# Two value products in one visit of the array, one copy for both, and other queues at the two passages of a hybrid attention layer

## The chip, the cores and the metric

The kernel runs on one core of a Trainium2 chip. The core has five engines with queues of their own: TensorE (PE), VectorE (DVE), ScalarE (ACT), GpSimd (POOL) and SyncE (SP). Each works through its queue in order; they meet through semaphores. SP here issues DMAs only; ACT and GpSimd issue some too. The metric is the device time of one execution in microseconds, and the median of several runs is compared.

## The reference

One layer of a decoder on 4096 tokens of width 1024, all in float32:

```python
h = rms_norm(x, norm_gain)                       # (4096, 1024)
qa, ka, va, ga, qr, kr, vr, gr = split(h @ w_in) # 4 x 512, 2 x 256, 2 x 512 columns
# 8 heads of 64: causal sliding window attention, three branches
for window, dilation in ((128, 1), (512, 4), (2048, 16)):
    s = q . k * 64**-0.5       # a query sees the 128 steps before it, at that dilation
    m, p = max(s), exp(s - max(s)); den = sum(p)
    o, lse = (p . v) / den, m + log(den)
attn = sum over branches of softmax(lse) * o
# 4 heads, key 64, value 128: retention in chunks of 128 with decay, then a norm per head
ret = group_norm(retention(qr, kr, vr)) * ret_gain
mixed = concat(silu(ga) * attn, silu(gr) * ret)
out = rms_norm(x + mixed @ w_out, final_gain)
```

Its products have a float32 result; the kernel splits operands of the large ones into a high part (hi) and a rest (lo) and adds three products (`mm3`, lines 46 to 50: hi·hi, hi·lo, lo·hi).

## The kernel before

It has three phases. **Phase 1** projects the tokens in 8 blocks of 512 to q, k, r (the q and k of retention) and the values, rotates q, k and r, and stores them to DRAM (`dr_q`, `dr_k`, `dr_r`, `dr_v`). **Phase 2** is the attention of 8 heads, with retention in 32 chunks as filler between. **Phase 3** computes the gates `g`, the mixed values `m`, the output projection `po` and the last norm.

In phases 1 and 2 the order of every engine is the order in which the program is written (`manual_schedule`). In phase 2 `attention()` is a generator that yields once per slot, and it returns the slot's planned cost in ns; `filler()` yields pieces of retention and of its values' projection with their costs; between two slots the planner takes pieces from the filler as long as the sum of costs lies below an even share per slot (`slot`). Phase 3's order is set by the framework.

A head has 24 groups (48 half-groups, one per slot; 384 slots in all): a group is four blocks of 128 queries, each against up to 256 keys, for one branch. In slot t the program writes, in this order: the scores of half-group t (`qk_bank`, tile S, L667), the transposes of the exponentials of half-group t−2 (`t_bank`, tile T, L704), in every second slot the product with the values of the group that ended two slots before (`pv_group`, tile O, L737), in the slots between the copy of O out of PSUM by ACT (`o_copy`: os for branches 0 and 1, L752; ob with a stride for branch 2, L759), the exponentials of half-group t−1 (`exp_row`, tile P, ACT, L695), a copy of T to SBUF (pt; ACT L714 for the second bank, DVE L716 for the first), and the row maxima of half-group t (`row_max`, DVE, L688). S has two PSUM buffers, T two, O one. The product uses the two halves of 64 columns of PE's array for the two banks.

At the passage from phase 1 to phase 2, SP's queue holds the first three and a half thousand columns of k for head 0 (`load_k`, L445, tile kk), the last stores of k, and the next chunk of x (hr, L423) for retention's values. The values' chunk (vch, L1037) is made from hr through hc.

At the passage from phase 2 to phase 3, the last head's statistics (st, L779, stored by SP to `dr_st` and loaded again to `raw`) lead to the branch weights (`dr_w`); the gates' weights wg0 and wg1 and the output weights wo are split to hi (ACT) and lo (GpSimd, or for every second wo DVE); e is the silu of a gate (ACT L1190) and m what goes into the projection.

Of the kernel before, what the change touches and what calls it, by code (L numbers as in the profile page):

```python
# [22 lines left out]
TRN = 109  # L23
# [7 lines left out]
H = 8  # L31
# [21 lines left out]
class Split:  # L53
# [22 lines left out]
    def split(self, j, lo_engine=None):  # L76
# [10 lines left out]
        self.nc.scalar.activation(hi, raw, AF.Copy)  # L87
# [27 lines left out]
def phase1(tc, io, dr, right, ahead):  # L115
# [5 lines left out]
    with ExitStack() as ctx:  # L121
# [203 lines left out]
        for b in range(NBLK):  # L325
# [40 lines left out]
            if last:  # L366
# [4 lines left out]
                kk = load_k(nc, kka, dr, 0, cols=slice(0, S - BLK))  # L371
# [172 lines left out]
def phase2(tc, io, dr, right, ahead, early3, raw, M):  # L544
# [3 lines left out]
    with ExitStack() as ctx:  # L548
# [34 lines left out]
        PT = [c2.tile([128, 8, 128], F32, name=f"pt{i}") for i in range(2)]  # L583
# [141 lines left out]
        def pv_group(it):  # L725

            h, br = it["h"], it["br"]
            o = psO.tile([128, 512], F32, tag="O", name="O2")
            ops = [pv_ops(it, bank) for bank in range(2)]
            for x in range(-max(map(len, ops)), 0):  # L730
                for bank in range(2):
                    if -x > len(ops[bank]):
                        continue
                    r, n, a, m, c0 = ops[bank][x]
                    idx = r * NB_OF[br] + n
                    need_v(h, br, idx // 8)
                    nc.tensor.matmul(  # L737
                        o[64 * bank : 64 * bank + 64, c0 : c0 + 128 * m],
                        vt[h, br, idx // 8][:, idx % 8, :],
                        it["pt"][:, a : a + m, :].rearrange("p a b -> p (a b)"),  # L740
                        start=-x == len(ops[bank]),
                        stop=x == -1,
                        skip_group_check=True,
                    )
            it["O"] = o

        def o_copy(it):
            h, br = it["h"], it["br"]
            r, n = it["blocks"][0]
            if br < 2:  # L750
                ob = osp.tile([128, 256], F32, tag="os", name="os2")
                nc.scalar.activation(ob, it["O"][:, :256], AF.Copy)  # L752
                c0 = n * 128 if br == 0 else r * 1024 + n * 128
                later(2, store_o, h, br, c0, 512, ob)
            else:
                if r % 4 == 0:
                    obuf[h] = ob16p.tile([128, 1024], F32, tag="ob16", name="ob16")

                nc.scalar.activation(  # L759
                    obuf[h].rearrange("p (m r) -> p r m", r=4)[:, r % 4, :], it["O"][:, :256], AF.Copy  # L760
                )
                if r % 4 == 3:
                    later(2, store_o, h, br, (r // 4) * 1024, 2048, obuf[h])

# [697 lines left out]
```

## Time and profile before

| what | value |
|---|---|
| median of three runs | 2415.1 us (2414.91 to 2417.89) |
| the profiled execution | 2416.7 us |
| its span | 2414.9 us |
| PE busy in the span | 2342.5 us, 97% |
| DVE, ACT, GpSimd busy | 62%, 41%, 30% |
| granted TensorE clock, mean | 0.988 |

Engine names are PE, PEld (weight loads), DVE, ACT, POOL; SPq, ACTq and POOLq are DMAs issued by that engine. A row of the timeline has the start in us from the start of the span, the duration, the engine, the line of the program, the operation, the tiles as out<-in, the shape and the number of instructions joined in it; in brackets stands the idle time of that engine before it and what ended the wait. A row of a group has the busy time in us, the mean of one in ns, and the idle time before them with its releasers. Rows of windows give a stretch and the busy time of each engine in it.

### The profile page before, as it was taken

What the parts mean: (1) busy time and instruction counts of PE and PEld (TensorE: products, weight loads), DVE (VectorE), ACT (ScalarE), POOL (GpSimd) and SP (SyncE); (2) the same over time, 40 slices, a digit from 0 to 9 for tenths busy, and PEclk for the clock granted to TensorE, in tenths of its full rate; (3) what the DMA queues carried; (4) which work ended last, traced back from release to release, by engine and by line L of the source; (5) the groups of instructions that cost most, each with busy time, mean ns of one, the idle gap of its engine ahead of it and who ended that gap; (6) DMA issues with size and microseconds to landing.
All of it is one profiled execution on the core that took longest, in us unless ns stands there. A gap on an engine that the chain in (4) does not pass through costs nothing. (4 is left out here: it accounts for less than half of the span.)

```text
span 2414.9 us, 41800 instructions
## 1 busy us (share of the span) xinstructions
PE 2342.5 (97%) x14568; PEld 1986.1 (82%) x14568; DVE 1485.8 (62%) x3923; ACT 990.0 (41%) x2865; POOL 725.0 (30%) x765
## 2 busy tenths in 40 slices
PE   7999999999997999999999999998899999999998
PEld 5778888888885888888888887877789899999997
DVE  5643543543534878787887879786665565665654
ACT  4322222222211666666666666667222222222221
POOL 5312112112112535353544535455221121121110
PEclk9999999999998999999999999999999999999999
DMA  6343343343356766758586765746575656656553
GB/s 192 130 145 107 133 144 107 133 144 111 129 147 202 165 163 139 181 131 189 131 180 148 169 156 131 176 125 196 143 182 154 145 171 152 145 168 154 142 153 92
DMA packets 404259, 362.59 MB, mean 150 GB/s; under 512 B 191848, under 2 KB 334824, under 8 KB 398928
## 3 DMA queue, kind: packets, MB, share of 16 engines
q1 hardware_dynamic: 389408, 332.91, 52.6%
q10 hardware_dynamic: 14112, 25.43, 3.4%
q8 instruction: 115, 1.88, 0.3%
q0 software_dynamic: 528, 1.58, 0.2%
q14 instruction: 96, 0.79, 0.1%
HBM read 241.18 MB, written 118.64 MB: 149 GB/s over the span
## 5 line engine op out<-in xcount | busy, mean ns | idle before, releaser
L688 DVE CUSTOM_DVE_ANT_0 S<-S,mask 128x256 f32<-128x256 f32 (+1 forms) x768 | 308.4, 402 | 156.7 <-PE S L667 123.5
L695 ACT ACTIVATE P<-S,nm 128x256 f32<-128x256 f32 (+1 forms) x768 | 337.2, 449 | 46.9 <-DVE nm L688 43.9
L50 PE MATMUL g<-h,wg 128*128 128x256 f32 x1024 | 290.6, 284 | 0.0
L704 PE MATMUL T<-ident,P 128*128 128x128 f32 x1368 | 213.3, 274 | 0.0
L49 PE MATMUL po<-wo,m 128*128 128x512 f32 x512 | 200.6, 392 | 0.0
L50 PEld LDWEIGHTS g<-h,wg 128*128 128x128 f32 x1024 | 197.1, 192 | 0.0
L737 PE MATMUL O<-pt,v 128*64 128x128 f32 (+1 forms) x1968 | 195.8, 325 | 0.0
L667 PE MATMUL S<-kk,qc 128*128 128x256 f32 x1024 | 186.9, 306 | 6.8 <-issue 2.8
L48 PE MATMUL po<-wohi,m 128*128 128x512 f32 x448 | 178.9, 399 | 6.9 <-ACT m L40 5.4
L1251 POOL TENSOR_TENSOR rs<-v,mhalf 128x1 f32<-128x1 f32 x32 | 17.5, 547 | 547.0 <-DVE v L1249 384.9
L667 PEld LDWEIGHTS S<-kk,qc 128*128 128x128 f32 x1024 | 150.0, 191 | 34.7 <-issue 17.5
L50 PE MATMUL po<-wohi,m 128*128 128x512 f32 x448 | 176.9, 396 | 0.2 <-DVE m L41 0.2
L172 POOL TENSOR_TENSOR sq<-sq,sq 128x512 f32<-128x512 f32 x56 | 76.3, 1362 | 331.4 <-ACT sq L168 331.4
L435 POOL TENSOR_TENSOR hc<-hr,hc 128x512 fp32r<-128x512 f32 x64 | 85.9, 1343 | 289.3 <-ACT hc L434 149.6
L737 PEld LDWEIGHTS O<-pt,v 128*64 128x64 f32 x1968 | 121.2, 137 | 60.3 <-issue 31.2
L704 PEld LDWEIGHTS T<-ident,P 128*128 128x128 f32 x1368 | 163.8, 141 | 0.2 <-ACT wg0hi L87 0.2
L695 ACT ACTIVATION_READ_ACCUMULATOR P<-S,nm 128x1 f32 x768 | 157.5, 205 | 0.0
L48 PE MATMUL g<-h,wg1hi 128*128 128x256 f32 x512 | 145.9, 286 | 4.6 <-ACT e L1190 4.5
L40 ACT ACTIVATE m<-e 128x256 fp32r<-128x256 f32 x128 | 53.1, 417 | 234.5 <-DVE e L1197 137.8
L49 PE MATMUL g<-h,wg1hi 128*128 128x256 f32 x512 | 146.9, 287 | 0.9 <-DVE h L483 0.7
L48 PE MATMUL g<-h,wg0hi 128*128 128x256 f32 x512 | 144.8, 283 | 1.8 <-ACT e L1190 1.8
L49 PE MATMUL g<-h,wg0hi 128*128 128x256 f32 x512 | 144.9, 283 | 0.0
(212 smaller groups left out, 6120.7 us busy)
## 6 DMA issues: line engine op xcount, KB each, us to landing
q<-dr_q SPq DMA_DIRECT2D x128, 256.0 KB
hr<-in_xT_dram SPq DMA_DIRECT2D x64, 512.0 KB
wb<-dr_w SPq DMA_DIRECT2D x128, 192.0 KB
o<-dr_o SPq DMA_DIRECT2D x192, 128.0 KB
v<-dr_v SPq DMA_DIRECT2D x94, 256.0 KB
xt<-in_xT_dram SPq DMA_DIRECT2D x64, 256.0 KB
dr_q<-hl SPq DMA_DIRECT2D x32, 512.0 KB
dr_k<-hl SPq DMA_DIRECT2D x32, 512.0 KB
```

The costliest lines, as they stand in the source:

```text
L40: nc.scalar.activation(dst[:, 0], src, AF.Copy)
L48: nc.tensor.matmul(out, wh, xh, start=first and i == 0, stop=False)
L49: nc.tensor.matmul(out, wh, xl, start=False, stop=False)
L50: nc.tensor.matmul(out, wl, xh, start=False, stop=last and i == n - 1)
L172: nc.gpsimd.tensor_tensor(sums[b], sums[b], sq, ALU.add)
L435: nc.gpsimd.tensor_tensor(hc[:, :, 1, :], src, hc[:, :, 0, :].bitcast(F32), ALU.subtract)
L667: nc.tensor.matmul(s[:, j * 256 : (j + 1) * 256], qq[h, t, half][:, off : off + 128] if br == 0 else it["q"][:, t, i, :], rhs, start=(j == ...
L688: nc.vector.tensor_tensor_reduce(sv, sv, mask[:, it["br"], c0:256], 1.0, BIG, ALU.add, ALU.min, accum_out=nm[:, col : col + 1])
L695: nc.scalar.activation(it["P", i // 2][:, i % 2, c0:256], sv, AF.Exp, bias=nm[:, col : col + 1], scale=-1.0, accum_out=den[:, col : col + 1])
L704: nc.tensor.transpose(t[:, j * 128 : (j + 1) * 128], it["P", bank][:, j // 2, j % 2 * 128 : j % 2 * 128 + 128], ident)
L737: nc.tensor.matmul(o[64 * bank : 64 * bank + 64, c0 : c0 + 128 * m], vt[h, br, idx // 8][:, idx % 8, :], it["pt"][:, a : a + m, :].rearran ...
L1251: nc.gpsimd.tensor_tensor(rs, v, mhalf, ALU.pow)
```

## The change

**The products of values.** `pv_group` becomes `pv_pair`: in every fourth slot (t % 4 == 2) the products of two groups are issued one behind the other, into one PSUM bank [128, 2, 256]. `o_copy` follows in the next slot, one ACT instruction of 512 columns for both. There are three PT tiles in place of two. The planned cost of a pair is 190 ns less than that of two groups, and an even share per slot falls accordingly.

**The passages.** The first load of k is issued by GpSimd in place of SP. The tile st is taken from the pool that also holds raw, and so are the tiles rb of phase 3. The last head's reloads of statistics are issued by ACT, from phase 3's start. Two loads of rt at the start of phase 3 are issued by GpSimd. All lo parts of wo are made by GpSimd, and the hi casts of wg0 by DVE in place of ACT.

```diff
@@ class Split @@
-    def split(self, j, lo_engine=None):
+    def split(self, j, lo_engine=None, hi_engine=None):
...
-        self.nc.scalar.activation(hi, raw, AF.Copy)
+        if hi_engine is None:
+            self.nc.scalar.activation(hi, raw, AF.Copy)
+        else:
+            hi_engine.tensor_copy(hi, raw)
         engine.tensor_tensor(self.lo[j], raw, hi.bitcast(F32), ALU.subtract)
@@ phase1 @@
-                kk = load_k(nc, kka, dr, 0, cols=slice(0, S - BLK))
+                kk = load_k(nc, kka, dr, 0, nc.gpsimd.dma_start, cols=slice(0, S - BLK))
@@ phase2 @@
-        PT = [c2.tile([128, 8, 128], F32, name=f"pt{i}") for i in range(2)]
+        PT = [c2.tile([128, 8, 128], F32, name=f"pt{i}") for i in range(3)]
...
-        def pv_group(it):
-            h, br = it["h"], it["br"]
-            o = psO.tile([128, 512], F32, tag="O", name="O2")
-            ops = [pv_ops(it, bank) for bank in range(2)]
...
-            it["O"] = o
+        def pv_pair(its):
+            o = psO.tile([128, 2, 256], F32, tag="O", name="O2")
+            for y, it in enumerate(its):
+                h, br = it["h"], it["br"]
+                ops = [pv_ops(it, bank) for bank in range(2)]
...
+                            o[64 * bank : 64 * bank + 64, y, c0 : c0 + 128 * m],
...
+            return o
-        def o_copy(it):
...
-                ob = osp.tile([128, 256], F32, tag="os", name="os2")
-                nc.scalar.activation(ob, it["O"][:, :256], AF.Copy)
-                c0 = n * 128 if br == 0 else r * 1024 + n * 128
-                later(2, store_o, h, br, c0, 512, ob)
+        def o_copy(its, o):
...
+                ob = osp.tile([128, 2, 256], F32, tag="os", name="os2")
+                nc.scalar.activation(ob, o, AF.Copy)
+                for y, it in enumerate(its):
+                    r, n = it["blocks"][0]
+                    c0 = n * 128 if br == 0 else r * 1024 + n * 128
+                    later(2, store_o, h, br, c0, 512, ob[:, y, :])
...
-                nc.scalar.activation(
-                    obuf[h].rearrange("p (m r) -> p r m", r=4)[:, r % 4, :], it["O"][:, :256], AF.Copy
-                )
-                if r % 4 == 3:
+                nc.scalar.activation(obuf[h].rearrange("p (m r) -> p r m", r=4)[:, r % 4 : r % 4 + 2, :], o, AF.Copy)
+                if r % 4 == 2:
...
-            st = r1.tile([96, 256], F32, tag="st", name="st2")
+            st = ahead["st"].tile([96, 256], F32, tag="st", name="st2")
...
-            later(3, load_stats, h)
+            if h < H - 1:
+                later(3, load_stats, h)
+            else:
+                ahead["stats"] = lambda: load_stats(h, nc.scalar.dma_start)
...
-                it["pt"] = PT[len(items) % 2]
+                it["pt"] = PT[len(items) % 3]
...
-                g = (t - 4) // 2 if t % 2 == 0 else -1
-                gp = (t - 5) // 2 if t % 2 else -1
+                a, ap = (t - 6) // 2, (t - 7) // 2
+                pair = items[a : a + 2] if t % 4 == 2 and 0 <= a < len(items) else None
+                paired = items[ap : ap + 2] if t % 4 == 3 and 0 <= ap < len(items) else None
...
-                if 0 <= g < len(items):
-                    pv_group(items[g])
-                    cost += pv_cost(items[g])
-                if 0 <= gp < len(items):
-                    o_copy(items[gp])
+                if pair:
+                    o = pv_pair(pair)
+                    cost += sum(map(pv_cost, pair)) - 190
+                if paired:
+                    o_copy(paired, o)
...
-            872 + TRN * (8 - ...) + pv_cost(it) for it in items[: len(groups)]
+            872 + TRN * (8 - ...) + pv_cost(it) - 95 for it in items[: len(groups)]
@@ phase3 @@
-            for _ in range(3):
+            for i in range(3):
+                if i == 2:
+                    ahead["stats"]()
                 yield
...
-                wo7.split(j, None if j % 2 else nc.gpsimd)
+                wo7.split(j, nc.gpsimd)
...
-                        rb = load_scales(nc, cp.tile([128, TB], F32, tag="rb", name="rb3"), dr, b + 1)
+                        rb = load_scales(nc, ahead["st"].tile([128, TB], F32, tag="rb", name="rb3"), dr, b + 1)
-                        heads[nb, nn] = load_heads(nb, nn, nc.scalar.dma_start if b == 0 and i == 0 else nc.sync.dma_start)
+                        heads[nb, nn] = load_heads(nb, nn, (nc.scalar, nc.gpsimd, nc.gpsimd)[i].dma_start if b == 0 and i < 3 else nc.sync.dma_start)
@@ body @@
-                wg[0].split(k, nc.gpsimd)
+                wg[0].split(k, nc.gpsimd, nc.vector)
...
-            ahead["rb"] = rawp.tile([128, TB], F32, name="rb3a")
+            ahead["rb"] = rawp.tile([128, TB], F32, tag="rb", name="rb3a")
+            ahead["st"] = rawp
```

The order of PE's queue in the middle of the attention phase, around products of values of branch 1 (S scores, T transposes, O the product, V, Ro, Rt, Rk and Rkv filler), before:

```order
L667 MATMUL S_8928<-kk_7355,qc_8804 128x256 x4
L704 MATMUL T_8933<-ident_5374,P_8867 128x128 x3
L737 MATMUL O_8937<-pt_5392,v_8618 64x128 x2
L737 MATMUL O_8937<-pt_5392,v_8618 64x256 x2
L737 MATMUL O_8937<-pt_5392,v_8618 64x128 x2
L667 MATMUL S_8953<-kk_7355,qc_8804 128x256 x4
L704 MATMUL T_8958<-ident_5374,P_8900 128x128 x4
L1015 MATMUL Rt_8970<-ident_5374,on_8664 128x128 x4
L48 MATMUL V_8657<-w2hi,hc_8669 128x512
L49 MATMUL V_8657<-w_5171,hc_8669 128x512
L50 MATMUL V_8657<-w2hi,hc_8669 128x512
L667 MATMUL S_8986<-kk_7355,qc_8864 128x256 x4
```

and with the change:

```order
L670 MATMUL S_8860<-kk_7316,qc_8732 128x256 x4
L707 MATMUL T_8865<-ident_5374,P_8796 128x128 x3
L742 MATMUL O_8869<-pt_5392,v_8638 64x128
L742 MATMUL O_8869<-pt_5392,v_8638 64x256 x2
L742 MATMUL O_8869<-pt_5392,v_8638 64x128 x2
L742 MATMUL O_8869<-pt_5393,v_8638 64x128 x2
L742 MATMUL O_8869<-pt_5393,v_8638 64x256 x2
L742 MATMUL O_8869<-pt_5393,v_8638 64x128 x2
L670 MATMUL S_8891<-kk_7316,qc_8732 128x256 x4
L707 MATMUL T_8896<-ident_5374,P_8828 128x128 x4
L670 MATMUL S_8913<-kk_7316,qc_8793 128x256 x4
L707 MATMUL T_8918<-ident_5374,P_8859 128x128 x4
```

Two products stand behind each other (of PT tiles 5392 and 5393), and the next product is two S further on; behind this pair S, T and S follow with no filler. On ACT's queue, the same place before:

```order
L752 ACTIVATE os_8582<-O_8553 128x256
L695 ACTIVATE P_8543,den_8475<-S_8544,nm_8474 128x256 x2
L714 ACTIVATE pt_5391<-T_8577 128x512
L695 ACTIVATE P_8571,den_8475<-S_8572,nm_8474 128x256 x2
L752 ACTIVATE os_8650<-O_8617 128x256
L695 ACTIVATE P_8606,den_8475<-S_8607,nm_8474 128x256 x2
L714 ACTIVATE pt_5392<-T_8645 128x512
L434 ACTIVATE hc_8669<-hr_8349 128x4x128
```

and with the change:

```order
L698 ACTIVATE P_8828,den_8413<-S_8829,nm_8412 128x256 x2
L757 ACTIVATE os_8901<-O_8869 128x512
L698 ACTIVATE P_8859,den_8413<-S_8860,nm_8412 128x256 x2
L717 ACTIVATE pt_5391<-T_8896 128x512
L698 ACTIVATE P_8890,den_8413<-S_8891,nm_8412 128x256 x2
L698 ACTIVATE P_8912,den_8413<-S_8913,nm_8412 128x128
L698 ACTIVATE P_8912,den_8413<-S_8913,nm_8412 128x256
L717 ACTIVATE pt_5392<-T_8957 128x512
```

The copy of O still stands ahead of the exponentials of the slot with the product, now once in four slots and 512 columns wide.

At the first passage, SP's queue before:

```order
L423 DMA hr_5113<-in_xT_dram 128x8x128
L445 DMA kk_5115<-dr_k 32x3584 x4
L259 DMA dr_k<-hl_5130 128x2x512
L259 DMA dr_k<-hl_5134 128x2x512
L423 DMA hr_5144<-in_xT_dram 128x8x128
L445 DMA kk_5115<-dr_k 32x512 x4
L1362 DMA rgain_5324<-in_ret_gain_dram 128x4
L423 DMA hr_5473<-in_xT_dram 128x8x128
```

and with the change:

```order
L262 DMA dr_k<-hl_5098 128x2x512
L426 DMA hr_5113<-in_xT_dram 128x8x128
L262 DMA dr_k<-hl_5130 128x2x512
L262 DMA dr_k<-hl_5134 128x2x512
L1373 DMA rgain_5324<-in_ret_gain_dram 128x4
L426 DMA hr_5144<-in_xT_dram 128x8x128
L448 DMA kk_5115<-dr_k 32x512 x4
L426 DMA hr_5474<-in_xT_dram 128x8x128
```

The four loads of 3584 columns of kk are gone from it; on GpSimd's queue they now stand ahead of the first lo parts of hc:

```order
L220 TENSOR_TENSOR tabR_4671<-tabR_4671,rb_4736 128x512 x2
L220 TENSOR_TENSOR tabA_4741<-tabA_4741,rb_4736 128x512 x2
L448 DMA kk_5115<-dr_k 32x3584 x4
L438 TENSOR_TENSOR hc_5138<-hr_5113,hc_5138 128x4x128
L438 TENSOR_TENSOR hc_5141<-hr_5113,hc_5141 128x4x128
masks.py:197 MEMSET ident_5374 128x128
L575 DMA mask_5379<-in_masks_dram 128x768
masks.py:199 AFFINE_SELECT ident_5374<-ident_5374 128x128
```

At the second passage, ACT's queue before:

```order
L1129 ACTIVATE junk_5326<-mhalf_5327 128x1
L779 ACTIVATE st_17656<-Ts_17653 96x256
L87 ACTIVATE wg0hi<-raw_17444 128x512
L752 ACTIVATE os_17683<-O_17658 128x256
L1163 DMA rt_17748<-dr_ret 128x256
L1163 DMA rt_17771<-dr_ret 128x256
L1190 ACTIVATE e_17773<-g_17512 128x256
L1190 ACTIVATE e_17777<-g_17551 128x256
L40 ACTIVATE m_17779<-e_17773 128x256
L40 ACTIVATE m_17787<-e_17777 128x256
L1190 ACTIVATE e_17785<-g_17587 128x256
```

and with the change:

```order
L1138 ACTIVATE junk_5326<-mhalf_5327 128x1
L784 ACTIVATE st_17395<-Ts_17392 96x256
L1172 DMA rt_17488<-dr_ret 128x256
L1172 DMA rt_17511<-dr_ret 128x256
L1199 ACTIVATE e_17513<-g_17254 128x256
L757 ACTIVATE os_17426<-O_17397 128x512
L40 ACTIVATE m_17519<-e_17513 128x256
L798 DMA raw_5321<-dr_st 16x2x256
L1199 ACTIVATE e_17517<-g_17299 128x256
L800 DMA raw_5321<-dr_st 16x4x64
L1199 ACTIVATE e_17525<-g_17333 128x256
L40 ACTIVATE m_17527<-e_17517 128x256
```

The casts wg0hi are gone from it; the reloads of the statistics (raw from dr_st) stand between the gates' silus e and the mixed values m.

More of the change, by code (lines that the diff above doesn't have):

```diff
@@ L723, in pv_ops @@
             return ([(r, n - 1, s0, 1, 0)] if n > 0 else []) + ops
-        def pv_group(it):
-            h, br = it["h"], it["br"]
-            o = psO.tile([128, 512], F32, tag="O", name="O2")
-            ops = [pv_ops(it, bank) for bank in range(2)]
[L730 to L743, printed above, removed]
-                    )
-            it["O"] = o
@@ L747, in o_copy @@
-        def o_copy(it):
-            h, br = it["h"], it["br"]
-            r, n = it["blocks"][0]
-            if br < 2:
-                ob = osp.tile([128, 256], F32, tag="os", name="os2")
-                nc.scalar.activation(ob, it["O"][:, :256], AF.Copy)
-                c0 = n * 128 if br == 0 else r * 1024 + n * 128
-                later(2, store_o, h, br, c0, 512, ob)
+        def pv_pair(its):
[3 more added lines that the diff above has]
+                ops = [pv_ops(it, bank) for bank in range(2)]
+                for x in range(-max(map(len, ops)), 0):
+                    for bank in range(2):
+                        if -x > len(ops[bank]):
+                            continue
+                        r, n, a, m, c0 = ops[bank][x]
+                        idx = r * NB_OF[br] + n
+                        need_v(h, br, idx // 8)
+                        nc.tensor.matmul(
+                            o[64 * bank : 64 * bank + 64, y, c0 : c0 + 128 * m],
+                            vt[h, br, idx // 8][:, idx % 8, :],
+                            it["pt"][:, a : a + m, :].rearrange("p a b -> p (a b)"),
+                            start=-x == len(ops[bank]),
+                            stop=x == -1,
+                            skip_group_check=True,
+                        )
+            return o
@@ L755, in o_copy @@
+        def o_copy(its, o):
+            h, br = its[0]["h"], its[0]["br"]
+            r, n = its[0]["blocks"][0]
+            if br < 2:
+                ob = osp.tile([128, 2, 256], F32, tag="os", name="os2")
[4 more added lines that the diff above has]
+                    later(2, store_o, h, br, c0, 512, ob[:, y, :])
             else:
@@ L1075, in phase2 @@
         per_head = sum(
-            872 + TRN * (8 - sum(it["blocks"][2 * i][1] == 0 for i in range(2))) + pv_cost(it) for it in items[: len(groups)]
+            872 + TRN * (8 - sum(it["blocks"][2 * i][1] == 0 for i in range(2))) + pv_cost(it) - 95 for it in items[: len(groups)]
         )
```

9 lines of the change are left out of this document (4 added, 5 removed).

## The prediction

> **What bounds the kernel now.** I read the share of the engines first, then the busy time by stages, then the order of time on PE.
>
> ```profile
> PE 2342.5 (97%) x14568; PEld 1986.1 (82%) x14568; DVE 1485.8 (62%) x3923; ACT 990.0 (41%) x2865; POOL 725.0 (30%) x765
> 740.00:800.00 60.00, 42.93 (x227) 35.69 (x227) 26.65 (x69) 14.98 (x38) 23.16 (x28) 0.86 0.74 193
> 800.00:1600.00 800.00, 795.14 (x6253) 667.89 (x6249) 643.50 (x2364) 548.88 (x1895) 362.70 (x410) 1.00 0.66 155
> 1600.00:1700.00 100.00, 81.31 (x603) 69.67 (x601) 70.57 (x192) 62.94 (x175) 58.44 (x59) 0.95 0.55 167
> ```
>
> The columns of the last three rows are the stretch, its length, and the busy time of PE, weight loads, DVE, ACT and GpSimd, then clock, DMA share and GB/s. PE is the bound: in the attention phase it is idle for 4.9 of 800 us, while DVE has 80% and ACT 69%. So time is won there only by giving PE less to do, and lost by any new wait of PE. Idle PE sits in the two passages: 60 − 42.9 = 17.1 us around 770, and 100 − 81.3 = 18.7 us in 1600 to 1700. The change touches all three places.
>
> A busy PE is not a PE at its peak, so I looked at what a slot of attention streams.
>
> ```profile
> 1002.02 0.60 PE L704 MATMUL T<-ident,P 128*128 128x128 f32 x4
> 1002.55 1.09 PE L737 MATMUL O<-pt,v 128*64 128x128 f32 x12
> 1003.57 0.74 PE L667 MATMUL S<-kk,q 128*128 128x256 f32 x4
> 1004.15 0.60 PE L704 MATMUL T<-ident,P 128*128 128x128 f32 x4
> 1004.59 0.60 PE L1015 MATMUL Rt<-ident,on 128*128 128x128 f32 x4
> ...
> 1009.54 0.39 PE L961 MATMUL Ro<-vch,stm 128*128 128x128 f32 x2
> 1009.68 0.72 PE L667 MATMUL S<-kk,q 128*128 128x256 f32 x4
> 1010.24 0.60 PE L704 MATMUL T<-ident,P 128*128 128x128 f32 x4
> 1010.77 0.97 PE L737 MATMUL O<-pt,v 128*64 128x128 f32 x9
> ...
> 1011.58 0.70 PE L969 MATMUL Rkv<-vch,kd 128*64 128x128 f32 x7
> ...
> 1012.80 0.60 PE L704 MATMUL T<-ident,P 128*128 128x128 f32 x4
> ```
>
> Starts show the stream better than durations, which overlap. Four transposes take 1004.59 − 1004.15 = 0.44 us, so 128 columns take 0.11. Ro's last two start at 1009.54 and need 0.22; S then has until 1010.24, which is 0.48 for four. A product of values (O) is 12 matmuls, 8 of 128 columns and 4 of 256, in the two halves of 64 columns of the array; 16 pieces of 0.11 would be 1.75 us, longer than the whole row, so the halves run side by side and the stream is 0.87. From the first T to the next T is 1004.15 − 1002.02 = 2.13, and 0.44 + 0.87 + 0.48 of that is accounted for. **0.34 us is lost** around the product. Is it lost per matmul or per visit? The second excerpt has a visit that also holds the eight Rkv of 64 columns (0.44 more; a few records are missing): 2.56 − 0.44 − 0.87 − 0.44 − 0.48 = 0.33. Half as much again in the visit, and the same loss: it belongs to going into the half-array mode and out of it.
>
> **The change, part by part.**
>
> *Fewer visits.* In the orders of the PE queue I count maximal runs of 64-column work (O, Rkv, or both in a row): 219 before, 128 after, which is 91 fewer. 91 x 0.34 = 31 us. The matmuls themselves, their number and their shapes stay. Bounds: 0 if the loss lay inside each group after all, 36 at 0.40. I take **−31**.
>
> *One copy instead of two, at the head of ACT's queue.* The pair's copy waits for the last of 24 matmuls, and the exponentials of the slot with the product stand behind it; the second S after the product needs the PSUM buffer that these exponentials read. Before, the same wait existed for every group:
>
> ```profile
> 1104.07 0.38 PE L942 MATMUL Rk<-ident,rk 128*128 128x128 f32 x2
> 1104.99 0.63 PE L667 MATMUL S<-kk,q 128*128 128x256 f32 x4
> 1103.17 0.38 ACT L752 ACTIVATE os<-O 128x256 f32<-128x256 f32 x1 [1.51 <-PE O L737]
> 1103.45 0.47 ACT L695 ACTIVATE P<-S,nm 128x256 f32<-128x256 f32 x1
> ...
> 1104.26 0.21 ACT L695 ACTIVATION_READ_ACCUMULATOR P<-S,nm 128x1 f32 x1
> 1104.35 0.60 ACT L714 ACTIVATE pt<-T 128x512 f32<-128x512 f32 x1
> ```
>
> O ends and its copy starts at 1103.17; the two exponentials end at 1104.47. PE had S and T done at 1104.07, where Rk starts, and would then have waited 0.4; filler (Rk, three V) covers it until 1104.99, and so S lost nothing. Over the phase such filler nearly always stands there:
>
> ```profile
> L752 ACT ACTIVATE os<-O 128x256 f32<-128x256 f32 x121 | 46.5, 384 | 124.6 <-PE O L737 124.4
> L759 ACT ACTIVATE ob<-O 128x256 f32<-128x256 f32 x56 | 35.8, 640 | 50.5 <-PE O L737 50.4
> L667 PE MATMUL S<-kk,qc 128*128 128x256 f32 x964 | 175.1, 305 | 4.7 <-POOL qc L648 2.0 <-ACT P L695 1.6 <-issue 1.0
> 1646.93 0.75 PE L667 MATMUL S<-kk,q 128*128 128x256 f32 x4 [1.59 <-ACT P L695]
> ```
>
> ACT idles 175 us at the head of its queue for O, and S pays 1.6 for it (the third row), but where filler has run out, in the phase's tail, S waits 1.59 for the exponentials (the fourth). After, the pair's slot already holds two products, and the planner, which evens out the slots, leaves less filler behind it. In the order of the change 62 pairs have the plain copy: behind 21 of them S, T, S stand with nothing between, behind 22 there are three V (0.7 us). The copy of 512 columns is not in the trace; it lies between 0.38 and 0.77 (one or two of today's), and the copy of a transposed bank, 512 columns wide on the same engine, took 0.60 (last row of the fence before), so I take 0.60, 0.22 longer than now. Without filler S then waits 0.40 + 0.22 = 0.62 us: 21 x 0.62 = 13. Behind three V it is about 0. The strided copy of two groups has bounds of 0.64 and 1.28; I take 1.1, so 0.72 more than a plain one now and a wait of 1.1 without filler, and with the filler that the order has behind those 29 pairs about 6 us in all. Sum **+19**; bounds 8 (copies at their lower bound, or PE late for other reasons) and 35.
>
> ACT itself has 96 copies in place of 192 and saves about 64 x 0.17 + 32 x 0.18 = 17 us; that is worth nothing where PE is the bound. The third PT buffer adds no instruction.
>
> *Passage to attention.* Rows around the gap:
>
> ```profile
> 779.50 0.79 PE L48 MATMUL V<-w2hi,hc 128*128 128x512 f32 x1 [16.47 <-DVE vch L1037]
> 778.36 0.43 DVE L432 CAST hc<-hr 128x512 fp32r<-128x512 f32 x1 [10.47 <-DMA hr<-in_xT_dram]
> 766.50 0.59 DVE L906 CAST qbd<-rq 64x256 fp32r<-64x256 f32 x2 [9.42 <-DMA rq<-dr_r]
> 735.76 18.08 SPq L445 DMA_DIRECT2D kk<-dr_k x4
> 761.79 2.72 SPq L259 DMA_DIRECT2D dr_k<-hl x2
> 767.95 0.37 SPq L423 DMA_DIRECT2D hr<-in_xT_dram x1
> 760.35 0.73 POOL L897 DMA_DIRECT2D rq<-dr_r x1
> 768.67 1.51 POOL L911 TENSOR_TENSOR qbd<-rq,qbd 64x256 fp32r<-64x256 f32 x2
> 778.92 1.27 POOL L435 TENSOR_TENSOR hc<-hr,hc 128x512 fp32r<-128x512 f32 x1 [8.75 <-DVE hc L432]
> ```
>
> PE waits 16.5 us for a cast that stands in DVE's order behind the one of hr, which landed 10.4 us after its issue at 767.95. That issue was late because SP's queue held four k transfers for 18 us, and the k stores behind them. With k on GpSimd's queue (idle then; its next own work is the lo part of hc) hr goes out earlier by about those 18 us and lands before 767. What is late next: rq, on GpSimd's queue in both, seen by DVE at 766.50. DVE then has qbd, rkh and the cast of hr behind each other, done by about 768.5; the lo part of hc stands on GpSimd behind qbd (768.67 + 1.51 = 770.18) and takes 1.27, to 771.45. Today it ends at 778.92 + 1.27 = 780.19, and the values need both parts. 780.19 − 771.45 is **−8.7**. Bounds: 0 if the four k transfers hold GpSimd's queue as they held SP's (18 us, from 735 to 754, with rq behind), −12 if rq lands earlier since less shares the DMA engines.
>
> The Trainium skill, page "SBUF — State Buffer", section "SBUF: two separate sides", speaks against it: a DMA issued from GpSimd has its descriptors written by GpSimd's cores, and these are locked out while VectorE runs certain two-port operations, by its example 3100 ns for 620. No run here shows it: rq was issued while DVE was idle. By it the four k issues would be five times as long (an estimate, 4 x 0.73 x 5 = 15 us from 735) and still end before GpSimd's next DMA, so the passage would gain the same.
>
> *Passage to the output phase.*
>
> ```profile
> 1674.47 0.66 ACT L1190 ACTIVATE e<-g 128x256 f32<-128x256 f32 x2 [6.37 <-DMA dr_st<-st]
> 1674.90 0.39 PE L48 MATMUL g<-h,wg1hi 128*128 128x256 f32 x1 [4.50 <-ACT e L1190]
> 1698.61 0.42 ACT L40 ACTIVATE m<-e 128x256 fp32r<-128x256 f32 x1 [6.35 <-DVE e L1197]
> 1699.09 0.79 PE L48 MATMUL po<-wohi,m 128*128 128x512 f32 x1 [5.42 <-ACT m L40]
> 1696.96 1.23 DVE L88 TENSOR_TENSOR wo<-wo,wohi 128x1024 fp32r<-128x1024 f32 x1 [2.50 <-POOL wo L88]
> 1651.43 1.12 PE L667 MATMUL S<-kk,q 128*128 128x256 f32 x4 [2.30 <-ACT P L695]
> ```
>
> e waits for the store of st because it takes st's memory; st in another pool removes 4.5 us of PE's wait. But the reloads of the statistics now issue from ACT between the e's, and ACT must wait there for the same store, which held e until 1674.47, while PE has part of another gate to do: I give back 2.0. DVE no longer takes turns with GpSimd in the lo parts of wo, which removes the 5.42 in front of po; the exponentials of the branch weights and the hi casts now stand ahead of an e on ACT, and I give back 2.7. The eight hi casts of wg0 leave ACT in the tail, where S waits for ACT 1.6, 1.6 and 2.3 us (the last row is one): 3 of these. Sum −2.5 − 2.7 − 3 = **−8**; bounds −14 and −2.
>
> **Sum:** −31 + 19 − 8.7 − 8 = −28.7. The profiled execution took 2416.7 with a span of 2414.9, so 2388 for such a run; the median of the runs, 2415.1, lies 1.6 below it, and I forecast **2387** (2386.4, rounded up).
>
> **The rivals.**
>
> *The copy behind the product decides (slower).* If the exponentials come later than I price, every pair loses more. A conversion of 0.63 (hc) or 0.69 (vch) standing in ACT's order between copy and exponential would do it. A delay of d falls on the 21 pairs without filler, the 22 with three V, and about 20 strided ones: 63 x d more. The sum is −28.7, so d = 0.45 us decides, and at 0.6 the time is 2387 + 38 = 2425. For it: the 175 us of idle at the head of ACT, and the row at 1646.93. Against: ACT is 31% idle, and the last row of S's group shows how little reaches PE with filler.
>
> *The wait never shows.* If PE's queue stays busy because S is late anyway and the loss of a visit moves into the wait, the +19 is 0 to 8: 2368 to 2376.
>
> *The passages do not gain.* k in GpSimd's queue holds rq as it held hr; the statistics come late and mixes wait for the branch weights. Then −31 + 19 alone: 2403.
>
> *The loss is not per visit.* Then the pairs only add waits: 2415.1 + 19 − 17 = 2417. The excerpt with Rkv speaks against it.
>
> **How the numbers follow.** The sum as it stands (2376 to 2398): 0.50. The wait never shows: 0.14. The passages fail: 0.18. The copy decides: 0.13. No gain per visit: 0.05. Of the runs here, 2414.9 to 2417.9, a change of 0.2% (4.8 us) can be told from none. The first three cases are faster, but for a little of the third (0.80 of 0.82); of the fourth 0.09 are slower and 0.04 within the bound, and the fifth is within it but for 0.01 slower: faster 0.80, same 0.10, slower 0.10. The range leaves out the slower ends and a little of the fast one: 2366 to 2411.
>
> **What would show it.** In the attention phase O's idle share on ACT stays, and S's group must show idle time released by ACT's P of some 20 us, in slots behind a pair that have no filler; the time between T rows around a pair should be about 0.34 shorter than two visits were. If S's idle time is under 8 us the second rival holds; over 45, the first. The first V behind the passage must stand near 771 with some 8 us of idle time before it; if it is still 16, the third. The gap before gate e near 1670 should be about 2 us. The forecast is wrong in its mechanism if the phase's PE busy time, visits being fewer, is no lower than before.

## The result and the profile after

The changed kernel takes 2438.3 us (median of 4 runs, 2433.3 to 2440.9), the kernel before 2415.0: **a ratio of 1.0094, with an interval of 1.0074 to 1.0114.** The forecast was 2387. The profiled execution of the change took 2433.3 with a span of 2431.2, that is 16.3 more than the span before, and the stages below are of that execution.

The page's row of the engines' busy time, then the busy time by stages, in the columns of the prediction:

```profile
PE 2329.4 (96%) x14568; PEld 1992.6 (82%) x14568; DVE 1485.4 (61%) x3928; ACT 977.8 (40%) x2761; POOL 724.1 (30%) x774
```

```profile
740.00:800.00 60.00, 47.33 (x251) 39.43 (x250) 29.16 (x83) 16.10 (x47) 26.74 (x31) 0.89 0.75 196
800.00:1600.00 800.00, 771.73 (x6166) 662.45 (x6165) 634.97 (x2327) 534.13 (x1781) 349.69 (x402) 1.00 0.67 153
1600.00:1700.00 100.00, 82.87 (x636) 72.85 (x635) 72.70 (x219) 61.48 (x173) 58.06 (x63) 0.92 0.59 174
```

PE is busy for 13 us less in all, and the kernel is longer all the same: PE waits. In 800 to 1600 it idles for 28.3 us where it idled for 4.9.

Stages are cut at the first S, the last S and the end of the span:

| kernel | first S at | first S to last S | last S to the end | span |
|---|---|---|---|---|
| before | 785.4 | 874.0 | 755.5 | 2414.9 |
| the change | 774.0 | 895.0 | 762.2 | 2431.2 |
| difference | −11.4 | +21.0 | +6.7 | +16.3 |

The first passage brings the first S forward as forecast; everything behind it loses.

**What S waits for.** The waits of PE's S and of DVE's cast of q, first S to last V, before:

```profile
PE S L667 <- POOL qc L648: 2.0, 1, 2.0
PE S L667 <- ACT P L695: 1.8, 5, 0.6
DVE qc L643 <- DMA raw<-dr_st: 2.5, 1, 2.5
DVE qc L643 <- DMA q<-dr_q: 2.4, 2, 2.1
```

and in the change, the largest:

```profile
PE S L670 <- ACT P L698: 23.3, 32, 4.1
PE S L670 <- POOL qc L651: 5.1, 7, 1.9
DVE qc L646 <- DMA raw<-dr_st: 9.9, 4, 3.2
```

Columns: the wait, its releaser, us in total, how often, the longest. The releaser "ACT P" hides two kinds of wait. One is the forecast one, at 1151:

```profile
1149.90 0.75 PE L670 MATMUL S<-kk,qc 128*128 128x256 f32 x4
1150.49 0.60 PE L707 MATMUL T<-ident,P 128*128 128x128 f32 x4
1151.66 0.71 PE L670 MATMUL S<-kk,qc 128*128 128x256 f32 x4 [0.57 <-ACT P L698]
1150.01 0.60 ACT L757 ACTIVATE os<-O 128x512 f32<-128x512 f32 x1 [2.36 <-PE O L742]
1150.50 0.47 ACT L698 ACTIVATE P<-S,nm 128x256 f32<-128x256 f32 x1
```

The copy of 512 columns takes 0.60 and holds the exponentials; with S, T and S on PE and nothing between, S waits 0.57. The price per wait was forecast as 0.62. The other kind is at the start of a head, at 1567:

```profile
1563.72 0.60 PE L707 MATMUL T<-ident,P 128*128 128x128 f32 x4
1564.25 1.95 PE L742 MATMUL O<-pt,v 128*64 128x128 f32 x22
1566.13 0.74 PE L670 MATMUL S<-kk,q 128*128 128x256 f32 x4
1566.70 0.60 PE L707 MATMUL T<-ident,P 128*128 128x128 f32 x4
1569.52 0.71 PE L670 MATMUL S<-kk,qc 128*128 128x256 f32 x4 [2.21 <-ACT P L698]
1566.24 0.60 ACT L757 ACTIVATE os<-O 128x512 f32<-128x512 f32 x1 [1.81 <-PE O L742]
1568.35 0.47 ACT L698 ACTIVATE P<-S,nm 128x256 f32<-128x256 f32 x1 [1.52 <-DVE nm L691]
1566.56 0.78 DVE L646 CAST qc<-q 128x512 fp32r<-128x512 f32 x1 [3.25 <-DMA raw<-dr_st]
1555.06 2.56 SPq L603 DMA_DIRECT2D q<-dr_q  x4
1563.25 0.32 SPq L798 DMA_DIRECT2D raw<-dr_st  x1
```

Read from S backwards: S waits for the exponential, that for DVE's row maximum, and DVE stood for 3.25 us in front of a cast of q. The program loads the second half of q two transfers per slot; the last four went out from 1555.1. The releaser named in the row is a small load that SP issued later; that the wait is for q was still an inference here, and the runs with q below test it. S's waits of over 0.1 us from the first S to the last V are 32.8 us in the change and 5.0 before. Sorted by such chains, 9.9 us in 25 waits have a copy at the head of ACT, 9.0 in 6 have DVE's wait for q, 7.8 in 10 an operation of GpSimd, and 4.1 is the one wait at 783 in the next fence. Before, the first three are 0, 1.0 and 2.0. All idle times of S below are counted over this stretch, from the trace of each run.

**The passages.** The first V of all, before:

```profile
757.30 0.50 PE L48 MATMUL V<-w2hi,hc 128*128 128x512 f32 x1 [0.60 <-ACT vo L273]
```

The same V, the V that stood at 779.50 before, and the gate behind the first projections, in the change:

```profile
770.36 0.50 PE L48 MATMUL V<-w2hi,hc 128*128 128x512 f32 x1 [0.84 <-DVE vch L1046]
769.55 0.75 DVE L1046 TENSOR_SCALAR vch<-V,rs_all 128x512 f32<-128x512 f32 x1 [4.72 <-PE V L50]
761.34 0.79 PE L48 MATMUL V<-w2hi,hc 128*128 128x512 f32 x1 [7.15 <-ACT vo L276]
760.60 0.69 ACT L276 ACTIVATE vo<-mm,rs_all 128x512 f32<-128x512 f32 x1 [10.83 <-DMA kk<-dr_k]
783.06 0.77 PE L670 MATMUL S<-kk,q 128*128 128x256 f32 x4 [4.09 <-ACT P L698]
1712.34 0.58 PE L49 MATMUL g<-h,wg1hi 128*128 128x256 f32 x1 [8.99 <-DVE h L486]
1696.23 15.78 POOL L91 TENSOR_TENSOR wo<-wo,wohi 128x1024 fp32r<-128x1024 f32 x6 [3.37 <-ACT wohi L88]
1696.81 2.67 DVE L525 TENSOR_TENSOR M<-raw 32x256 f32<-32x256 f32 x1
```

The gap of 16.5 us in front of 779.50 is down to 0.84 in front of 770.36, and in its place stand 7.2 ahead of the first V of all and 4.1 ahead of an S, both for ACT. By the releasers that the profile infers, ACT stood ahead of the first V between its own stores of values until a load of k had landed; ahead of that S it had stood 14.8 us in front of a cast of the next x chunk, whose load SP issued only at 772.1. At the second passage a new gap of 9 us stands in front of a gate that needs h of the second block.

### The profile page after: what moved, and what is told of

It reads as the page before. It is cut to its first block, busy times and chain, and to the rows that moved or that the text cites. A ratio compares the mean times of both kernels' runs of the same rounds, so it can differ in the third digit from the quotient of the medians.

```text
span 2431.2 us, 41520 instructions
## 1 busy us (share of the span) xinstructions
PE 2329.4 (96%) x14568; PEld 1992.6 (82%) x14568; DVE 1485.4 (61%) x3928; ACT 977.8 (40%) x2761; POOL 724.1 (30%) x774
## 5 line engine op out<-in xcount | busy, mean ns | idle before, releaser
L670 PE MATMUL S<-kk,qc 128*128 128x256 f32 x1024 | 188.4, 308 | 26.7 <-ACT P L698 15.7
L742 PE MATMUL O<-pt,v 128*64 128x128 f32 (+1 forms) x1968 | 174.7, 320 | 0.0
L742 PEld LDWEIGHTS O<-pt,v 128*64 128x64 f32 x1968 | 126.1, 137 | 41.9 <-issue 16.5
```

What stands on the lines that cost most here:

```text
L670: nc.tensor.matmul(s[:, j * 256 : (j + 1) * 256], qq[h, t, half][:, off : off + 128] if br == 0 else it["q"][:, t, i, :], rhs, start=(j == ...
L742: nc.tensor.matmul(o[64 * bank : 64 * bank + 64, y, c0 : c0 + 128 * m], vt[h, br, idx // 8][:, idx % 8, :], it["pt"][:, a : a + m, :].rear ...
```

## The experiments

Ratios are to the kernel before on the same chip, with their intervals; spans are of the profiled execution, which can lie some us off the median.

### Which part loses

`pairs_alone` undoes all edits of the passages; `passages_alone` is the kernel before with these edits and products one group at a time.

> The products in pairs with the passages as before. If the loss lies in the attention phase (the traces of before and of the change: 21 us longer from the first S to the last S, of which 4 are one wait at the start), this costs 10 to 17 us: 2425 to 2432. If it lies in the passages, the pairs are worth what fewer visits save less the waits forecast, and the time is 2400 to 2410.

> All edits of the passages, products one group at a time as before. If the loss lies in the attention phase: the first passage gives 5 to 9 us, the second takes 5 to 9, so 2411 to 2419. If it lies in the passages: 2430 or more. If only the meeting of both costs, both this and the pairs alone are at 2415 or below.

Pairs alone: 2429.6 us, 1.0063 (1.0050 to 1.0076). Passages alone: 2420.1, 1.0033 (1.0020 to 1.0046). Both lose. First S to last S takes 889.7 with the pairs alone (+15.7) and 877.5 with the passages alone; last S to the end takes 755.4 and 763.4 (+7.9). So the attention phase's loss belongs to the pairs, that of the output phase to the passages' edits, and the first passage's gain of 10 us at the first S is down to 6 at the last S. The passages alone lie 1 us above the range forecast for this case.

### The copy behind the exponentials

```diff
-                if paired:
-                    o_copy(paired, o)
                 if i1:
                     exp_row(i1, 2 * b1)
                     exp_row(i1, 2 * b1 + 1)
+                if paired:
+                    o_copy(paired, o)
```

> The whole change, but on ACT the copy of a pair's O stands behind the two exponentials of its slot in place of ahead of them. If the head of ACT's queue is what S waits for, S's idle time in the attention phase falls from 33 to under 12 us and the time by 15 to 22, to 2416 to 2423. If S waits for other things (casts of q on DVE, DMAs that land late), S's idle time stays above 22 and the time above 2428.

2432.5 us, 1.0076 (1.0057 to 1.0096), which the whole change's interval overlaps. The 25 waits with a copy at ACT's head are gone, but S's idle time is 28.0 in place of 32.8: DVE's waits for q rose from 13.5 to 19.6 us. **My theory, that this one wait was the loss, fell here.** A wait had stood in front of another one.

### The loads of q at once

In the program, the loads of the second half of q go out two per slot. Here they all go out at the head's first slot, on the pairs alone:

```diff
-                                qq[h, i, 1] = load_q(nc, qp, dr, h, i, 1, soon)
+                                qq[h, i, 1] = load_q(nc, qp, dr, h, i, 1)
```

> The pairs alone, but the eight loads of the second half of q are issued at once at a head's start, not two per slot. If DVE's casts of q wait at each head's start because these loads are issued late (10 us of S's 30 us of idle time, by my sorting of the rows), that part falls below 4 and the time from 2429.6 to 2418 to 2424. If the transfers themselves limit it, the waits stay and the time is above 2427.

2427.7 us, 1.0060 (1.0048 to 1.0073), 2 us below the pairs alone and above the expected range. DVE's waits for q vanish (11.9 to 0 us), which shows that these were waits for q, and late issue their cause; S's idle time falls from 28.9 to 22.8. The six middle heads fall from 660.9 to 654.5 us, counted from one head's first S to the next one's. But the first head grows from 107.5 to 116.7, and `pairs_q` below, which leaves the first head's loads as they were, has 107.4 there: at the passage it costs time to put these loads into SP's queue at once.

### Filler spread evenly

```diff
                     o = pv_pair(pair)
-                    cost += sum(map(pv_cost, pair)) - 190
+                if 0 <= (t - 4) // 2 < len(items):
+                    cost += (pv_cost(items[(t - 4) // 2]) - 95) / 2
```

> The pairs alone, but the planned cost of a pair is spread evenly over the four slots it serves, so that filler stands behind every pair. If S waits because the slots behind a pair have no filler to cover the copy of O and the exponentials, the waits with a copy at the head of ACT (10 us) fall below 4, S's idle time from 29 to under 20, and the time to 2414 to 2422. If the idle time only moves to the casts of q, it is 2426 or more.

2423.7 us, 1.0040 (1.0028 to 1.0052): 6 us better than the pairs alone, but 2 above the expected range. No wait with a copy at ACT's head is left, and S still idles for 26.7: DVE's waits for q rose from the 11.9 of the pairs alone to 16.4.

Three edits each took one of the two waits away, and S's idle time stayed at 23 to 28 us. (The expectation below says 28 for all three; with q at once it was 22.8.) Either there is a common bound, or the waits stand behind one another.

### Two waits taken away together

`pairs_exp_q` has the copy behind the exponentials and q at once, the latter from the second head on (the first keeps its two per slot). `pairs_even_exp_q` has the even filler too, and `before_exp_q` is the control without pairs.

```diff
-                                qq[h, i, 1] = load_q(nc, qp, dr, h, i, 1, soon)
+                                qq[h, i, 1] = load_q(nc, qp, dr, h, i, 1, None if h else soon)
```

> The pairs alone; the copy of O behind the exponentials, and from the second head on the second half of q issued at once: two of the waits taken away together. Taken away one at a time, S's idle time stayed at 28 us. If one wait only hides the next, both together bring it under 16 and the time from 2429.6 to 2414 to 2421. If a common bound (DVE's row maxima in the slots without filler, two buffers of S) keeps it near 28, the time is 2425 or more.

> As pairs_exp_q, and the planned cost of a pair spread over its four slots. If the waits are lined up one behind the other (copy, q, and slots without filler in which DVE is late), S's idle time falls under 12 us, the six middle heads take 640 to 648 us (652 before, 661 with the pairs alone) and the time is 2405 to 2414. If not, 2420 or more.

> The kernel before with the copy of O behind the exponentials and q at once, products one group at a time. S waits 5 us in all there, so both theories expect no change beyond 3 us: 2410 to 2415. A gain of 5 or more would mean that these edits are worth something by themselves, and that the two runs beside this one say less about the pairs.

`pairs_exp_q`: **2401.9 us, 0.9944 (0.9931 to 0.9957)**, faster than both kernels and better than either theory allowed. S idles for 10.7. `pairs_even_exp_q`: 2410.3, 0.9976 (0.9967 to 0.9985); its six middle heads take 647.0, as expected, but S idles for 15.6, so the even filler gives nothing once the other two are gone, and costs 8. The control: 2420.2, 1.0019 (1.0008 to 1.0031). It is 5 us slower than the kernel before, where I allowed 3: T now waits for DVE, which it does not do in the kernel before. Which of the two edits brings this wait was not tested.

```profile
PE T L704 <- DVE pt L716: 7.2, 9, 1.3
```

So the gain is not that of the two edits by themselves; it needs the pairs.

To fill in the two missing cells, each edit was then made alone on the pairs:

> The pairs alone with the copy of O behind the exponentials, nothing else. Both edits together gave 28 us (2429.6 to 2401.9). If the wait for q takes the place of the one removed, this gives less than 8 of them: 2422 to 2430. If the copy alone is most of it and the passages hid that in the earlier run on the whole change, 2402 to 2412.

> The pairs alone with the second half of q issued at once from the second head on; the first head's loads stay as they were, since in the earlier run they cost that head 9 us. If the two waits stand behind each other, this gives about the 6.5 us that the six middle heads showed there and a part of the first head's: 2418 to 2424, and the two edits are worth more together than added. If q alone is most of it, 2402 to 2412.

| on the pairs alone | median us | ratio and interval | S idles, us | of it for the copy | of it for q |
|---|---|---|---|---|---|
| nothing | 2429.6 | 1.0063 (1.0050 to 1.0076) | 28.9 | 10.2 | 7.6 |
| copy behind the exponentials | 2425.6 | 1.0044 (1.0029 to 1.0059) | 26.3 | 0 | 17.8 |
| q at once from the second head | 2420.9 | 1.0037 (1.0024 to 1.0050) | 21.5 | 11.9 | 0 |
| both | 2401.9 | 0.9944 (0.9931 to 0.9957) | 10.7 | 0 | 0 |

Alone 4 and 9 us, together 28. (The cells ran on three chips; by the ratios it is 5, 6 and 29. The intervals of the two single edits overlap or touch that of nothing, so their sizes are rough.) The last columns show the masking: with the copy out of the way, the wait for q takes more than its place, 17.8 us in place of 7.6. Three rows of windows show the rest. They hold the same work, first S to last V. The first is of the copy alone:

```profile
782.00:1624.00 842.00, 814.84 (x6494) 705.95 (x6494) 667.97 (x2456) 567.66 (x1868) 373.76 (x431) 0.98 0.67 153
```

The second is of q alone, the third of both edits:

```profile
783.60:1616.50 832.90, 811.13 (x6491) 696.91 (x6490) 670.53 (x2459) 558.21 (x1869) 373.27 (x429) 1.00 0.67 155
```

```profile
783.00:1597.50 814.50, 802.83 (x6490) 696.43 (x6490) 667.06 (x2459) 568.85 (x1869) 374.77 (x429) 1.00 0.69 158
```

With q late, the copy alone leaves 27.2 us of idle PE, and its busy time is 12 higher than with both edits for the same matmuls, at a mean clock of 0.98. (The profiled executions were the slowest of six for the copy alone and the fastest of six for both, so the 27.5 us between these rows are 4 more than between the medians.) A lowered clock makes its waits cost more than they last. In the timeline of the copy alone, and in its stretches of 4 us around it:

```profile
912.11 1.19 PE L667 MATMUL S<-kk,qc 128*128 128x256 f32 x4 [4.24 <-ACT P L695]
```

```profile
908.00:912.00 4.00, 0.00 (x0) 0.00 (x0) 2.62 (x9) 1.05 (x5) 0.00 (x0) 0.75 0.23 42
912.00:916.00 4.00, 3.89 (x14) 3.52 (x15) 2.30 (x9) 2.77 (x10) 0.00 (x0) 0.50 0.95 251
916.00:920.00 4.00, 4.00 (x29) 3.37 (x29) 3.24 (x11) 1.62 (x5) 1.12 (x1) 0.89 0.52 131
```

After a wait of 4.2 us the clock stands at 0.50, and the four S take 1.19 in place of 0.72. Summed over stretches of 4 us from 804 on, the lowered clock takes 12.0 us in the copy alone, 3.4 in the pairs alone and in the change, 1.7 before, and nothing in `pairs_q` and `pairs_exp_q`; part of it falls in time in which PE waits anyway, as in the first of the three stretches. In the copy alone the clock fell behind each of the five waits of 1.93 us and longer. Not every such wait does it: in the change one of 2.21, at 1569.5, leaves it at 1.00. The Trainium skill, "TensorE: Matmul & The Clock Gate", section "HAM oscillation — how this bites in real kernels", gives the rule that PE should have no idle gaps of more than about 3.4 us. Of the five waits here only one, of 4.24, was longer than that; the other four, of 1.93 to 3.21, lowered the clock too.

The clock is not all of it. With q alone it was at 1.00, as with both edits, and PE's busy time is 8 us higher all the same, with 45 waits of S in place of 17. That is about 0.3 us a wait beyond the idle time that the rows show (an estimate from these two traces); what makes it up was not tested.

### The parts of the passages

> Only the first load of k goes to GpSimd's queue, all else as before. If what the first passage gained in the run of all passages (first S 10 us, last S 6 us earlier) comes from k alone, the time is 2405 to 2409. If the gap only moves ahead of the first V, where ACT's copy waits for a DMA, and S then waits for ACT, it is 2411 to 2415.

2412.6 us, 0.9997 (0.9988 to 1.0006): no change. The first S comes 7.6 us earlier, the first head then takes 113.0 in place of 107.6 us, and the last S is 4.2 earlier. The gap has moved:

```profile
765.27 0.80 PE L48 MATMUL V<-w2hi,hc 128*128 128x512 f32 x1 [9.16 <-ACT vo L273]
764.53 0.69 ACT L273 ACTIVATE vo<-mm,rs_all 128x512 f32<-128x512 f32 x1 [10.48 <-DMA kk<-dr_k]
```

The second passage's edits, first with the turns at wo given back to the whole change, then with the loads of rt given back to the passages alone, then three of them one at a time on the kernel before:

> The whole change, but GpSimd and DVE take turns at the lo parts of wo, as before. If DVE's chain to h of the second block (2 to 3 us for small operations while GpSimd runs six lo parts without a break) makes the gap of 9 us near 1703, the gap falls below 4 and the time by 4 to 8, to 2430 to 2434. If the late statistics make it, the gap stays and the time is 2436 to 2440.

> All edits of the passages but the two loads of rt by GpSimd, products one group at a time. In the order of PE the gates of the second block then stand behind the first projections again, as before the change. If that order makes the gap of 7 us near 1689, the loss behind the last S (8 us in the run of all passages) falls to 2 or less and the time from 2420 to 2409 to 2414. If DVE and GpSimd in each other's way make it, the loss stays and the time is 2417 or more.

> Before, but GpSimd makes all lo parts of wo. The order of PE is that of before. My forecast was a gain of 2.7 us or more from it (no turns between DVE and GpSimd in front of po). If instead DVE's small operations wait out GpSimd's operations (2.7 us for one of 0.6 in the trace of the change), the branch weights come later and the time is unchanged or up: 2413 to 2419; a gain would show as 2408 to 2411.

> Before, but st in the pool of raw and the last statistics loaded by ACT in phase 3's start. Forecast: the wait of 4.5 us before the gate goes and 2 come back: 2409 to 2412. If ACT's wait for the store and the later branch weights take it back, the behind-last-S stretch is not shorter than 755 us and the time 2413 to 2418.

> Before, but two loads of rt by GpSimd. The framework then orders PE's queue otherwise (gates of the second block ahead of the first projections, as in the change). If this order makes the gap before h, the stretch behind the last S grows by 3 to 8 us: 2417 to 2422. If not, 2412 to 2415.

| run | edit | median us | ratio and interval | last S to the end |
|---|---|---|---|---|
| wo_turns | the change, lo parts of wo by turns | 2435.3 | 1.0085 (1.0068 to 1.0102) | 759.4 |
| passages_but_rt | all passages, rt by SP | 2418.2 | 1.0021 (1.0011 to 1.0031) | 758.8 |
| wo_alone | before, lo parts of wo all by GpSimd | 2414.5 | 1.0001 (0.9992 to 1.0010) | 755.6 |
| st_alone | before, st in raw's pool, reloads by ACT | 2416.6 | 1.0006 (0.9997 to 1.0014) | 758.2 |
| rt_alone | before, two loads of rt by GpSimd | 2422.1 | 1.0030 (1.0019 to 1.0041) | 763.4 |

**The two loads of rt lose the most:** 0.3% alone, and the stretch behind the last S is as long as with all edits of the passages (763.4; before 755.5). Phase 3's order is set by the framework. With these loads on GpSimd the trace has 169 matmuls of gates between the last S and the first po in place of 144: a gate of the second block now comes before the first projections, and waits for its h. In the run `rt_alone`:

```profile
1688.80 0.58 PE L48 MATMUL g<-h,wg1hi 128*128 128x256 f32 x1 [5.85 <-ACT h L482]
1695.36 0.58 PE L49 MATMUL g<-h,wg1hi 128*128 128x256 f32 x1 [3.41 <-DVE h L483]
```

The wait of 4.5 us before e does go when st leaves r1's memory (st_alone has none there). But its time is not shorter; five waits of 0.8 to 2.9 stand among the po that follow. The turns at wo neither gain nor lose where the order stays; given back to the change, they leave a gap of 6.6 of the 9.0, and the time lies between the two ranges of its expectation. `passages_but_rt` lies 2 us below `passages_alone`, with overlapping intervals, in the range forecast for the rival, and loses 0.2% still; its gates stand as before, so some of the passages' loss is in other edits, and this was not taken further apart (the hi casts of wg0 by DVE have no run of their own).

### The whole change with both waits taken away

> The whole change, with the copy of O behind the exponentials and, from the second head on, q at once. The pairs with these two edits were at 2402, and the edits of the passages cost 5 us where products go one group at a time. If both add, 2405 to 2409, and the change with two lines moved is faster than before. If the second passage's gaps grow with earlier work, 2411 or more.

2409.0 us, 0.9979 (0.9968 to 0.9991): at the end of the expected range, faster than before, and 7 above the pairs without the passages. The best kernel found is `pairs_exp_q` at 0.9944: the pairs, the copy one place further back, q issued at once, and the passages as they were.

## Why the prediction was wrong

From the first S to the last V the change takes 849.0 us, before 832.4. PE's busy time there falls by 12, where −31 was forecast, and its idle time rises by 28, where +19 was. **The step that failed is the sum over the attention phase:** it took the copy's wait for the only new one, put the wait for q at a head's start at nothing without a reason (1.0 us of S's idle time before, 9.0 in the change), and charged each wait at its idle time. The runs showed a second wait behind the first, and a price above the idle time. The two passages, forecast at −16.7, came out as a loss by themselves (1.0033).

**The loss per visit (−31): right in kind, a little large.** `pairs_exp_q` has the same matmuls between first S and last V as the kernel before, in 802.8 us of busy PE; before it was:

```profile
785.00:1618.00 833.00, 827.93 (x6492) 695.78 (x6491) 669.86 (x2460) 567.55 (x1961) 378.65 (x428) 1.00 0.66 155
```

The difference is 25.1, of which 1.7 is the clock of the kernel before, for 207 − 121 = 86 visits in these stretches: 0.27 each, not 0.34. Over 91 visits that is −25. In the change itself busy PE falls by 12 only; the lowered clock (3.4 us there) and some 0.3 us for each of its 49 waits are of the size of what is missing.

**The copy at ACT's head (+19): the mechanism right, and the sum wrong.** As idle time the copy's waits are 9.9 us, half the forecast. As a price they are about 4 us while q is late, and some 20 once q is early (2420.9 to 2401.9), where their 11.9 us of idle time go and PE's busy time falls by 8. That the +19 meets this last figure is luck: the forecast meant idle time. Luck too is the sign named beforehand, some 20 us of S's idle time released by ACT's P: it came out at 23.3, but less than half of that is the copy's. The forecast also took for granted that the rest of the phase had room. The profile before showed that DVE stood for 4.9 us in front of casts of q and that S paid 1.0 of it; the prediction never looked at what limits the start of a head, where the loads of the second half of q begin only with the head and then go out two per slot. With the pairs S pays 7.6 to 9.0 for it, and 7 to 8 for GpSimd's operations, where it was 2.0. The argument behind it, DVE at 80% and ACT at 69% and so room for both, is an average over the phase and says nothing of the slots at a head's start.

**The rivals.** The slower one, the copy behind the product, gave 2425 and asked for a delay of 0.45 us or more per pair. Its place was right for 10 of 33 us. The other wait, for a transfer late at each head, was not among the rivals. Neither decides by itself: 4 and 9 us alone, 28 together.

**The tail (−3) came out as a loss.** With the pairs alone the last head takes 121.4 us up to its last S, before 114.1. Behind the last V, where no such filler is left, S idles for 10.6 us in place of 7.7. The hi casts that I counted on were off ACT in the change, and the last head still took 119.5.

**The first passage (−8.7): right in number up to the first S, and no time.** The V forecast near 771 came at 770.4, and PE's first S 7.6 to 11.4 earlier. It did not come by the forecast chain: DVE's vch no longer waited for hr or rq, but 4.7 us for V itself, which ACT had held, so the agreement is in part luck. The step that failed is "what is late next: rq": next was ACT, whose stores of values, by the releasers that the profile infers, wait for one of the loads of k that SP still issues. It holds the first V of all by 7.2 us in the change and 9.2 in `k_alone`, where it was 0.6. Then ACT is late again, in front of the first head's exponentials, for the next chunk of x.

**The second passage (−8): wrong.** I priced every edit against the order of before. The order of PE, which the prediction had compared only around the products, puts a gate of the second block first: the two loads of rt, which the sum did not price at all, cost 7.9 us behind the last S by themselves. The edits that it did price gained nothing alone (wo 755.6, st 758.2, before 755.5). The waits of ACT on the statistics, priced at 2.0 and 2.7, were not what decided.

## What to carry to other kernels

Where several waits stand behind each other, taking away one can show the next at a greater length: remove them together before dropping a theory, and compare the idle time of the stalled engine by cause, not only the run time. Before saving work on the engine that bounds, look at the places where every period starts anew (a new head, a new buffer) and ask what arrives there, how late, and how much earlier it could be issued. Where the order is left to a framework, read the new order at every place the edit touches: moving two small loads changed which matmuls came first.

## What the runs showed of the hardware

A wait of PE cost more than its length. In `pairs_exp` waits of 1.9 to 4.2 us were each followed by some us at half clock, 12.0 us by the sum above; in other runs single waits of 1.9 to 2.2 were not. Between `pairs_q` and `pairs_exp_q`, both at full clock, each wait went with some 0.3 us more of busy time.

DVE's small operations waited out GpSimd's large ones. In the change the sum M of 32x256 (0.61 before) took 2.67 and 2.69 while GpSimd ran its six lo parts of wo, 2.6 each, without a break, and in the kernel before one such sum took 2.73 where a lo part ran beside it:

```profile
1683.80 2.73 DVE L523 TENSOR_TENSOR M<-M,raw 32x256 f32<-32x256 f32 x1
1683.28 2.78 POOL L88 TENSOR_TENSOR wo<-wo,wohi 128x1024 fp32r<-128x1024 f32 x1 [6.03 <-ACT wohi L87]
```

The Trainium skill, "SBUF — State Buffer", section "SBUF: two separate sides", has this as an exclusive lock on a port pair that the two share, held for the whole instruction, for DVE operations with two inputs in SBUF among others. The rows agree: DVE's sum ends 0.5 us behind the end of GpSimd's operation. Whether DMAs issued by GpSimd suffer in the same way, the prediction's place on that page, stays open: the four loads of k went out in 2.2 us while DVE was busy, but DVE's operations there read a matmul's result; none was a copy within SBUF.

Going into half-array matmuls and out of them cost 0.27 us a visit (23.4 us of busy PE over 86 visits).
